# First group of gate products: two weight blocks split under the last plain gate, u's sums in another order, weight sums from their own copy

## The chip, the cores and the metric

The kernel runs on one core of a Trainium2 chip. The metric is the device time of one execution in microseconds; lower is better. A core has TensorE (matrix products, into PSUM), VectorE and ScalarE (elementwise work), GpSimd (called POOL in the profile) and SyncE (called SP), and 16 DMA engines that all queues share. SP and POOL issue nearly all transfers here. A transfer that adds to its target (accumulate) is issued by POOL.

## The reference

One layer of a streaming encoder in float32, 512 frames of 1024 channels. The part that matters here is the merge of three branches:

```python
u = rmsnorm(h, g_mix[l])
proj = u @ w_in[l]
...
y_mem = o_mem.reshape(B, S, MEM_W) @ w_mem_o[l]
gt = jax.nn.sigmoid(gates.reshape(B, S, N_BRANCH, D))
merged = gt[:, :, 0] * y_gla + gt[:, :, 1] * y_fox + gt[:, :, 2] * y_mem
h = h + merged @ w_out[l]
```

The gates are 3 x 1024 columns of `u @ w_in`. A squared-ReLU MLP and a last norm follow.

## The kernel before, in words

**Precision.** Each float32 operand is split into two float32r parts: a ScalarE cast gives hi, a VectorE subtraction gives lo. A product is three matmuls (`mm3`, lines 155 to 157): hi x hi, hi x lo, lo x hi, where the first named is the weight (for a product of u: L155 and L156 read whi, L157 reads wlo). For a block of 128x1024 weights `split_w` does this (cast L145, subtraction L146). `split` (L208, L209) does it for other operands. The raw blocks, whi and wlo each have three buffers that go round, so the cast of a block waits until the third block before it has been used by TensorE.

**Plain gates.** The eight tiles of the FoX gate are plain products `u @ w` with 512 columns (`gT`). The last four run in the GLA stage, woven between the GLA steps by `weave`: after each step, so many units of gate work as its share says (a unit is three matmuls).

**Gate groups.** The other two gates (mem, then gla) are done in four groups of 512 output channels (`gate_group`). Each group replaces an eight-block 2x2 product by a Strassen-Winograd scheme of seven products over half the channels and half the frames, numbered 1 to 7, 24 matmuls of 256 columns each. The left operands are blocks of u (products 1, 2, 4) and sums of them (5, 6, 3, 7, called S1, S2, S4, S3). They are made once, for the first group: `xsum[1]` and `xsum[3]` are computed in the GLA stage (`u_sum`), and `gate_lefts` splits `xsum[1]` into S1 (tiles f0h, f0l), then twice subtracts and adds in place and splits (S2 is f1, S4 is f2), and splits `xsum[3]` into S3, which overwrites a block of u that the plain gates no longer need. The weight operands are blocks ("11", "12", "21", "22") and running sums of them: `total` (wb) starts as 11, and accumulating DMAs make it 11+12, 11+12+22, 11+12+22+21; `other` is 12+22. Each add into `total` must wait until the value before it has been split. Between the products stand the branch's four outputs (`output(j)`: 12 matmuls of 512 columns against `w_mem_o`). `take` sums the products into the gate, `merge` multiplies by the output, and POOL adds to `acc`.

In the first group before, the order on TensorE is 1, 2, output, output, 5, 3, 6, 7, output, 4, output; in the others it is 1, 2, output, 5, output, 3, 6, 7, output, 4, output.

**Who sets the order.** TensorE's order is that of the code. On the other engines and queues a scheduler orders the instructions when the kernel is built; `tc.issue_after(x)` keeps what stands under it behind x. Each engine then works its own list strictly in that order.

**T sums.** `next_sum` hangs a DMA on the cast of every third weight block or so: these make sums of MLP weight blocks in DRAM (tiles T), on POOL's queue.

Of the kernel before, what the change touches and what calls it, by code (L numbers as in the profile page):

```python
# [14 lines left out]
ALU = mybir.AluOpType  # L15
# [49 lines left out]
def hybrid_block(ctx, tc, chunks, wst, memT, xN, cols, gffn, gfin, wup, cst, out):  # L65
    nc = tc.nc
# [24 lines left out]
    def f(ap):  # L91
        return ap.bitcast(F32)
# [27 lines left out]
    chunk_n, cast_now = [0], [None]  # L120

    def next_sum(after):

# [18 lines left out]
    def split_w(raw):  # L142
        hi = wp.tile([P, 1024], F32R, tag="hi", name=nm("whi"))
        lo = wp.tile([P, 1024], F32R, tag="lo", name=nm("wlo"))
        cast = nc.scalar.copy(hi, raw)  # L145
        nc.vector.tensor_tensor(lo, raw, f(hi), op=ALU.subtract)  # L146
# [575 lines left out]
    with pool("gla") as lp:  # L722
# [123 lines left out]
        def u_sum(n):  # L846
# [4 lines left out]
            nc.vector.tensor_tensor(x, x, al, op=ALU.add)  # L851
            nc.vector.tensor_tensor(x, x, bl, op=ALU.subtract)

        xsum = {}
        A11, A12, A21, A22 = ([f(t[:, 4 * k:4 * k + 4, 256 * i:256 * i + 256]) for t in (uhi, ulo)] for i in range(2) for k in range(2))

        steps = (
            (decays, 0, 13), (key_turn, 0, 3), (gla_scores, 0, 3), (states, 0, 3), (gla_scores, 1, 3), (gla_values, 0, 3),
            (gla_values, 1, 3), (decays, 1, 3), (gla_turn, 0, 4), (gla_turn, 1, 4), (key_turn, 1, 3), (gla_scores, 2, 3),
            (states, 1, 3), (u_sum, 1, 0), (gla_scores, 3, 3), (gla_values, 2, 3), (gla_values, 3, 4), (u_sum, 3, 0), (gla_turn, 2, 3),  # L860
            (gla_turn, 3, 3))
        weave([partial(fn, i) for fn, i, _ in steps], 64, *[gla_g(j) for j in range(4)], fox_late(), shares=[n for *_, n in steps])
    gst.close()

# [23 lines left out]
    with pool("outp") as op_:  # L888
# [8 lines left out]
        GATE = {1: [t[:, 0:4, 0:256] for t in (uhi, ulo)], 2: [t[:, 4:8, 0:256] for t in (uhi, ulo)],  # L897
                4: [t[:, 4:8, 256:512] for t in (uhi, ulo)], 5: S1, 6: S2, 3: S4, 7: S3}

        def gate_lefts():  # L900

            split(*S1, xsum[1])
            for to, (ah, al) in ((S2, A11), (S4, A12)):
                nc.vector.tensor_tensor(xsum[1], ah, xsum[1], op=ALU.subtract)
                nc.vector.tensor_tensor(xsum[1], xsum[1], al, op=ALU.add)
                split(*to, xsum[1])
            split(*S3, xsum[3])

        loaded = [None]

        def gate_group(gate, wo, oh, ol, i, lefts=None, last=None):
            src = {b: wst[index["W", gate, i, b]] for b in ("11", "12", "21", "22")}
            total, other = (h_tile(2 * (i % 2) + n, "wb") for n in range(2))
            X = [op_.tile([P, 2, S], F32, tag=f"ct{n}", name=nm("ct")) for n in range(2)]
            (c11, c21), (c12, c22) = ([x[:, :, 256 * n:256 * n + 256] for n in range(2)] for x in X)
            nc.sync.dma_start(total, src["11"])
            first = nc.sync.dma_start(other, src["12"]).ins

            def plus(to, b):
                nc.gpsimd.dma_start(to, src[b], accum_op=ALU.add)  # L920

            def block(b):
                raw = wp.tile([P, 1024], F32, tag="raw", name=nm("raw"))
                with tc.issue_after(first):
                    loaded[0] = nc.sync.dma_start(raw, src[b]).ins
                return raw

            def vec(to, x, y, op=ALU.add):
                nc.vector.tensor_tensor(to, x, y, op=op)

            def tanh(x):
                nc.scalar.activation(x, x, AF.Tanh, scale=0.5)

            def product(n, raw):
                wh, wl = (t.rearrange("p (a k c) -> p a k c", a=2, k=4) for t in split_w(raw))
                uh, ul = GATE[n]
                ps = mmt([P, 2, 256])
                for a in range(2):
                    for k in range(4):
                        mm3(ps[:, a, :], wh[:, a, k, :], wl[:, a, k, :], uh[:, k, :], ul[:, k, :], k == 0, k == 3)  # L940
                return ps

            def take(n, ps):
                if n == 1:
                    nc.scalar.copy(c21, ps)
                if n == 2:
                    vec(c11, c21, ps)
                    tanh(c11)
                if n == 5:
                    nc.scalar.copy(c22, ps)  # L950
                if n == 6:
                    vec(c21, c21, ps, ALU.subtract)
                    vec(c22, c22, c21, ALU.subtract)
                if n == 3:
                    vec(c12, c22, ps)
                    tanh(c12)
                if n == 7:
                    vec(c22, c22, ps, ALU.subtract)
                    tanh(c22)
                    vec(c21, c21, ps)  # L960
                if n == 4:
                    vec(c21, c21, ps)
                    tanh(c21)

            ys = {}

            def output(j):
                if j % 2 == 0:
                    ys["w"] = get_o(wo, j)
# [12 lines left out]
            j = 4 * i  # L982
            take(1, product(1, total))
            plus(total, "12")
            plus(other, "22")
            take(2, product(2, block("21")))
            if lefts is not None:
                lefts()
            output(j + 2)
            if lefts is not None:  # L990
                output(j + 3)
            take(5, product(5, total))
            plus(total, "22")
            if lefts is None:
                output(j + 3)
            p3 = product(3, block("22"))
            take(6, product(6, total))
            plus(total, "21")
            take(3, p3)
            take(7, product(7, other))  # L1000
            merge(j + 2)
            merge(j + 3)
            output(j)
            take(4, product(4, total))
            merge(j)
            output(j + 1)
            merge(j + 1)

        gate_group("gate_mem", "w_mem_o", omh, oml, 0, lefts=gate_lefts)
# [437 lines left out]
```

## Time and profile before

| | |
|---|---|
| median of 3 runs | 852.09 us (850.49 to 853.2) |
| the profiled execution | 849.31 us, span 847.5 us, clock 0.991 |
| TensorE busy | 827.2 us, 98% of the span |
| VectorE, ScalarE, POOL busy | 607.0, 461.2, 107.1 us |
| DMA | 155.61 MB in packets, mean 184 GB/s |
| chain that ended last | TensorE 88%, VectorE 6%, DMA 2% |

A row of a timeline gives start and duration in us, engine, line of the code, operation, output<-input, shape, and in brackets the idle time of the engine before it with what ended it. PE is TensorE, PEld its weight loads, DVE VectorE, ACT ScalarE. Windows give the busy us of each engine in a stretch, then PEclk (the granted TensorE clock as a share of full speed), the busy share of the DMA engines and GB/s. Matmul ends are modelled, so distances between starts say more than durations.

### The profile page before, as it was taken

The numbers are of one execution on the slowest core, as the hardware profiler recorded it, in microseconds if no ns is written. First come the engines' busy times: TensorE is split into PE (matmuls) and PEld (weight loads), VectorE is DVE, ScalarE is ACT, GpSimd is POOL, SyncE is SP. The second block draws the span as 40 slices with busy tenths as digits, with TensorE's granted clock in tenths as the row PEclk, the third lists the DMA queues.
The fourth block names the chain that finished last, engine by engine and source line by source line (L and its number), as shares of the span: only waits on it lengthen the run. The fifth ranks groups of instructions, "written<-read, shape, count | busy, mean of one in ns | idle before, by whom it ended". The sixth has DMA issues, their size and how long they took to land.

```text
span 847.5 us, 12609 instructions
## 1 busy us (share of the span) xinstructions
PE 827.2 (98%) x4841; PEld 723.1 (85%) x4841; DVE 607.0 (72%) x953; ACT 461.2 (54%) x723; POOL 107.1 (13%) x130
## 2 busy tenths in 40 slices
PE   8999999999999999899999999999999999999995
PEld 6888888888888787789999889998998899889984
DVE  5846887665456684764766846887589678877897
ACT  6765777543354231443444535775577467646754
POOL 1000000001002111132422300001001100110011
PEclk9999999999999999999999999999999999999998
DMA  8524654538666474679998531978857875796543
GB/s 312 189 99 151 178 173 124 179 128 238 180 216 159 129 216 120 166 204 234 270 273 213 168 112 33 279 210 192 243 187 157 221 242 165 188 244 201 151 83 116
DMA packets 39181, 155.61 MB, mean 184 GB/s; under 512 B 4880, under 2 KB 5840, under 8 KB 37072
## 3 DMA queue, kind: packets, MB, share of 16 engines
q1 hardware_dynamic: 28144, 96.06, 31.7%
q0 software_dynamic: 9472, 54.53, 30.5%
q10 hardware_dynamic: 1504, 4.21, 1.3%
q8 instruction: 38, 0.62, 0.3%
q14 instruction: 23, 0.19, 0.1%
HBM read 152.65 MB, written 31.49 MB: 217 GB/s over the span
## 4 chain that ended last, share of the span: by engine, by line
PE 88%; DVE 6%; DMA 2%; issue 2%; ACT 1%; POOL 0%; SPq 0%; POOLq 0%; DVEq 0%; ACTq 0%
PE mm L155 22%; PE mm L157 22%; PE mm L156 22%; PE a L156 5%; PE a L155 5%; PE a L157 5%; DVE h L1117 1%; PE a L801 1%; DVE wlo L146 1%; DMA xn<-in_xN_dram 1%; DVE lo L209 1%; DMA wb<-in_wst_dram 1%; PE a L521 1%; DMA raw<-in_wst_dram 1%; PE a L818 1%
## 5 line engine op out<-in xcount | busy, mean ns | idle before, releaser
L155 PE MATMUL mm<-uhi,whi 128*128 128x512 f32 (+1 forms) x352 | 126.9, 360 | 3.1 <-ACT whi L145 3.1
L157 PE MATMUL mm<-uhi,wlo 128*128 128x512 f32 (+1 forms) x352 | 124.6, 354 | 0.9 <-DVE wlo L146 0.9
L156 PE MATMUL mm<-ulo,whi 128*128 128x512 f32 (+1 forms) x352 | 124.4, 353 | 0.0
L146 DVE TENSOR_TENSOR wlo<-raw,whi 128x1024 fp32r<-128x1024 f32 x67 | 87.4, 1308 | 36.9 <-ACT whi L145 36.7
L145 ACT CAST whi<-raw 128x1024 fp32r<-128x1024 f32 x67 | 70.2, 1049 | 67.2 <-PE mm L156 42.5
L208 ACT CAST hi<-raw 128x1024 fp32r<-128x1024 f32 x65 | 68.2, 1049 | 47.4 <-PE mm L156 34.3
L209 DVE TENSOR_TENSOR lo<-raw,hi 128x1024 fp32r<-128x1024 f32 x65 | 79.5, 1223 | 18.7 <-ACT hi L208 18.7
L155 PEld LDWEIGHTS mm<-uhi,whi 128*128 128x128 f32 x352 | 67.3, 191 | 12.6 <-ACT whi L145 3.6
L157 PEld LDWEIGHTS mm<-uhi,wlo 128*128 128x128 f32 x352 | 67.3, 191 | 10.3 <-DVE wlo L146 1.2
L156 PEld LDWEIGHTS mm<-ulo,whi 128*128 128x128 f32 x352 | 67.4, 191 | 8.0
L208 ACT CAST hi<-b 128x1024 fp32r<-128x1024 f32 x40 | 42.0, 1049 | 41.4 <-PE mm L157 26.9
L156 PE MATMUL mm<-lo,ch 128*128 128x512 f32 x160 | 62.5, 391 | 0.9 <-DVE lo L209 0.9
L157 PE MATMUL mm<-u2h,lo 128*128 128x256 f32 x224 | 63.4, 283 | 0.0
L156 PE MATMUL mm<-u2l,hi 128*128 128x256 f32 x224 | 63.4, 283 | 0.0
L155 PE MATMUL mm<-u2h,hi 128*128 128x256 f32 x224 | 63.4, 283 | 0.0
L157 PE MATMUL mm<-hi,cl 128*128 128x512 f32 x160 | 62.3, 389 | 0.0
L155 PE MATMUL mm<-hi,ch 128*128 128x512 f32 x160 | 62.3, 389 | 0.0
L209 DVE TENSOR_TENSOR lo<-b,hi 128x1024 fp32r<-128x1024 f32 x40 | 48.8, 1222 | 18.2 <-ACT hi L208 18.2
L1301 POOL DMA_DIRECT2D b<-in_wst_dram x32 | 27.3, 854 | 272.5 <-DVE lo L209 201.8
L155 PE MATMUL mm<-u2sh,hi 128*128 128x256 f32 x168 | 47.5, 283 | 0.0
L156 PE MATMUL mm<-u2sl,hi 128*128 128x256 f32 x168 | 47.5, 283 | 0.0
L157 PE MATMUL mm<-u2sh,lo 128*128 128x256 f32 x168 | 47.5, 283 | 0.0
(412 smaller groups left out, 2163.5 us busy)
## 6 DMA issues: line engine op xcount, KB each, us to landing
raw<-in_wst_dram SPq DMA_DIRECT2D x113, 512.0 KB
b<-in_wst_dram POOLq DMA_DIRECT2D x32, 512.0 KB, 5.5
raw<-T SPq DMA_DIRECT2D x28, 512.0 KB
T<-in_wst_dram POOLq DMA_DIRECT2D x12, 1024.0 KB, 9.4
wb<-in_wst_dram POOLq DMA_DIRECT2D x16, 512.0 KB, 5.7
b<-in_wst_dram SPq DMA_DIRECT2D x16, 512.0 KB
wb<-in_wst_dram SPq DMA_DIRECT2D x8, 512.0 KB
nFb<-dF ACTq DMA_DIRECT2D x6, 512.0 KB
```

The source lines that it names most:

```text
L145: cast = nc.scalar.copy(hi, raw)
L146: nc.vector.tensor_tensor(lo, raw, f(hi), op=ALU.subtract)
L155: nc.tensor.matmul(ps, lh, rh, start=start, stop=False)
L156: nc.tensor.matmul(ps, lh, rl, start=False, stop=False)
L157: nc.tensor.matmul(ps, ll, rh, start=False, stop=stop)
L208: nc.scalar.copy(hi, src)
L209: return nc.vector.tensor_tensor(lo, src, f(hi), op=ALU.subtract).ins
L521: nc.tensor.matmul(ps[:, :w], q, K[e][:, 0, :w], start=True, stop=False)
L801: nc.tensor.matmul(ps[:, t, :], kk[:, sl], qq[:, sl], start=True, stop=True)
L818: nc.tensor.matmul(po[r, t, :], qpos[e][:, 64 * c:64 * c + 64], prev[:, c, :], start=False, stop=True)
L1117: nc.vector.tensor_tensor(to, to, x, op=op)
L1301: nc.gpsimd.dma_start(to[i], wst[index["B", q, i, x]], accum_op=ALU.add)
```

## The change

It touches the first group alone in its order of work, and a few dependences in all four.

- The first two weight blocks ("11" and "21") are loaded and split in the GLA stage (`gate_ready`, ahead of the last `gla_turn`, with no share of gate work), by SP and with the usual buffers. `ready` hands them to products 1 and 2.
- `total` is still loaded with block 11, as a copy of its own, so its first add doesn't wait for a split.
- `lefts_1` splits S1, then S3; `lefts_2` makes S2 after product 5's split, and S4 after product 6's split.
- The products of the first group come as 1, 2, output, output, 5, 7, 6, output, 3, 4, output.
- Adds are issued in the order of the code, the load of each `w_mem_o` block after the first two loads of its group, and the split of `total` for products 6 and 4 after the cast just before it.
- `decays(1)` has one more share of gate work.

```diff
-        nc.vector.tensor_tensor(lo, raw, f(hi), op=ALU.subtract)
+        low_now[0] = nc.vector.tensor_tensor(lo, raw, f(hi), op=ALU.subtract).ins
...
+        def gate_ready(b):
+            ready.append(get_w(("W", "gate_mem", 0, b)))
...
-            (gla_values, 1, 3), (decays, 1, 3), (gla_turn, 0, 4), (gla_turn, 1, 4), (key_turn, 1, 3), (gla_scores, 2, 3),
+            (gla_values, 1, 3), (decays, 1, 4), (gla_turn, 0, 4), (gla_turn, 1, 4), (key_turn, 1, 3), (gla_scores, 2, 3),
...
-            (gla_turn, 3, 3))
+            (gate_ready, "11", 0), (gate_ready, "21", 0), (gla_turn, 3, 3))
...
-        def gate_lefts():
...
+        def lefts_1():
+            cast = nc.scalar.copy(S1[0], xsum[1]).ins
+            nc.vector.tensor_tensor(S1[1], xsum[1], f(S1[0]), op=ALU.subtract)
+            with tc.issue_after(cast):
+                split(*S3, xsum[3])
+
+        def lefts_2(to, block):
+            with tc.issue_after(low_now[0]):
+                nc.vector.tensor_tensor(xsum[1], block[0], xsum[1], op=ALU.subtract)
+                nc.vector.tensor_tensor(xsum[1], xsum[1], block[1], op=ALU.add)
+                cast = nc.scalar.copy(to[0], xsum[1]).ins
+                nc.vector.tensor_tensor(to[1], xsum[1], f(to[0]), op=ALU.subtract)
+            return cast
...
+            before = summed[0]
             def plus(to, b):
-                nc.gpsimd.dma_start(to, src[b], accum_op=ALU.add)
+                with tc.issue_after(before) if before is not None else ExitStack():
+                    summed[0] = nc.gpsimd.dma_start(to, src[b], accum_op=ALU.add).ins
...
                 if j % 2 == 0:
-                    ys["w"] = get_o(wo, j)
+                    with tc.issue_after(first):
+                        ys["w"] = get_o(wo, j)
...
-            take(1, product(1, total))
+            if ready is None:
+                take(1, product(1, split_w(total)))
             plus(total, "12")
             plus(other, "22")
-            take(2, product(2, block("21")))
-            if lefts is not None:
-                lefts()
+            if ready is not None:
+                take(1, product(1, ready[0]))
+            take(2, product(2, ready[1] if ready else split_w(block("21"))))
+            if ready is not None:
+                with tc.issue_after(low_now[0]):
+                    lefts_1()
             output(j + 2)
...
-            take(5, product(5, total))
+            w = split_w(total)
+            cast = cast_now[0]
+            take(5, product(5, w))
             plus(total, "22")
-            if lefts is None:
+            if ready is not None:
+                cast = lefts_2(S2, A11)
+                p7 = product(7, split_w(other))
+            else:
                 output(j + 3)
-            p3 = product(3, block("22"))
-            take(6, product(6, total))
+                p3 = product(3, split_w(block("22")))
+            with tc.issue_after(cast):
+                w = split_w(total)
+            take(6, product(6, w))
             plus(total, "21")
+            if ready is not None:
+                cast = lefts_2(S4, A12)
+                output(j)
+                p3 = product(3, split_w(block("22")))
             take(3, p3)
```

What the lists of the engines hold at three places, before and now. The first is VectorE at the start of the first group. x_3056 is `xsum[1]`, f0, f1, f2 are S1, S2, S4, wb_3239 is `total`, raw_3277 block 21, raw_3323 the first output's weights. Before:

```order
L209 TENSOR_TENSOR f0l_3234<-x_3056,f0h_3233 128x1024
L146 TENSOR_TENSOR wlo_3246<-wb_3239,whi_3245 128x1024
L904 TENSOR_TENSOR x_3056<-uhi,x_3056 128x1024
L905 TENSOR_TENSOR x_3056<-x_3056,ulo 128x1024
L146 TENSOR_TENSOR wlo_3280<-raw_3277,whi_3279 128x1024
L146 TENSOR_TENSOR wlo_3326<-raw_3323,whi_3325 128x1024
L209 TENSOR_TENSOR f1l_3236<-x_3056,f1h_3235 128x1024
L904 TENSOR_TENSOR x_3056<-uhi,x_3056 128x1024
L905 TENSOR_TENSOR x_3056<-x_3056,ulo 128x1024
L929 TENSOR_TENSOR ct_3241<-ct_3241,mm_3284 128x2x256
```

Now raw_3317 is the first output's weights, wb_3252 `total`, wb_3253 `other`, mm_3286 product 2, mm_3417 product 6, raw_3449 the third output's weights, raw_3468 block 22:

```order
L943 TENSOR_TENSOR ct_3254<-ct_3254,mm_3286 128x2x256
L146 TENSOR_TENSOR wlo_3320<-raw_3317,whi_3319 128x1024
L146 TENSOR_TENSOR wlo_3350<-wb_3252,whi_3349 128x1024
L914 TENSOR_TENSOR x_3056<-uhi,x_3056 128x1024
L146 TENSOR_TENSOR wlo_3385<-wb_3253,whi_3384 128x1024
L915 TENSOR_TENSOR x_3056<-x_3056,ulo 128x1024
L917 TENSOR_TENSOR f1l_3249<-x_3056,f1h_3248 128x1024
L146 TENSOR_TENSOR wlo_3414<-wb_3252,whi_3413 128x1024
L914 TENSOR_TENSOR x_3056<-uhi,x_3056 128x1024
L146 TENSOR_TENSOR wlo_3452<-raw_3449,whi_3451 128x1024
L146 TENSOR_TENSOR wlo_3471<-raw_3468,whi_3470 128x1024
L915 TENSOR_TENSOR x_3056<-x_3056,ulo 128x1024
```

and right behind these:

```order
L943 TENSOR_TENSOR ct_3254<-ct_3254,mm_3417 128x2x256
L943 TENSOR_TENSOR ct_3255<-ct_3255,ct_3254 128x2x256
L917 TENSOR_TENSOR f2l_3251<-x_3056,f2h_3250 128x1024
L146 TENSOR_TENSOR wlo_3509<-wb_3252,whi_3508 128x1024
L943 TENSOR_TENSOR ct_3255<-ct_3255,mm_3474 128x2x256
```

The splits of blocks 11 and 21 have left this place for the GLA stage, the sum of product 2 has moved ahead of the first output's wlo, and the sums of u stand further back, between the splits of weights.

The second place is ScalarE in the same stretch: before, from the last plain gate's tanh on,

```order
L632 ACTIVATE th_3221<-mm_3174 128x512
L208 CAST og_2580<-og_3208 128x512
L208 CAST f0h_3233<-x_3056 128x1024
L145 CAST whi_3245<-wb_3239 128x1024
L145 CAST whi_3279<-raw_3277 128x1024
L145 CAST whi_3325<-raw_3323 128x1024
L208 CAST f1h_3235<-x_3056 128x1024
```

and now from product 1's copy on (mm_3260 is product 1, mm_3353 product 5):

```order
L959 COPY ct_3254<-mm_3260 128x2x256
L145 CAST whi_3319<-raw_3317 128x1024
L946 ACTIVATE ct_3254<-ct_3254 128x2x256
L145 CAST whi_3349<-wb_3252 128x1024
L145 CAST whi_3384<-wb_3253 128x1024
L964 COPY ct_3255<-mm_3353 128x2x256
L916 CAST f1h_3248<-x_3056 128x1024
L145 CAST whi_3413<-wb_3252 128x1024
```

Product 1's cast no longer follows the tanh; the cast of f1 now stands behind the copy of product 5 and ahead of product 6's cast.

The third place is POOL's list between the last GLA norm and the first merges: before,

```order
L215 TENSOR_TENSOR rr_3150<-ms_3149,cst_s 128x4
L920 DMA wb_3240<-in_wst_dram 128x1024
L920 DMA wb_3239<-in_wst_dram 128x1024
L132 DMA T_3_87<-in_wst_dram 16x16384
L920 DMA wb_3555<-in_wst_dram 128x1024
L920 DMA wb_3239<-in_wst_dram 128x1024 x2
```

and now:

```order
L215 TENSOR_TENSOR rr_3150<-ms_3149,cst_s 128x4
L132 DMA T_3_87<-in_wst_dram 16x16384
L934 DMA wb_3252<-in_wst_dram 128x1024
L934 DMA wb_3253<-in_wst_dram 128x1024
L934 DMA wb_3252<-in_wst_dram 128x1024 x2
L934 DMA wb_3557<-in_wst_dram 128x1024
```

The 1 MB copy to T now stands ahead of the first group's adds; wb_3555 and wb_3557 are the next group's `other`. On SP the two early loads stand ahead of the loads of `total` and `other`.

More of the change, by code (lines that the diff above doesn't have):

```diff
@@ L119, in hybrid_block @@
     sums = sum_ops()
-    chunk_n, cast_now = [0], [None]
+    chunk_n, cast_now, low_now = [0], [None], [None]
     def next_sum(after):
@@ L852, in u_sum @@
             nc.vector.tensor_tensor(x, x, bl, op=ALU.subtract)
+        ready = []
+        def gate_ready(b):
+            ready.append(get_w(("W", "gate_mem", 0, b)))
         xsum = {}
@@ L898, in hybrid_block, with gate_group @@
                 4: [t[:, 4:8, 256:512] for t in (uhi, ulo)], 5: S1, 6: S2, 3: S4, 7: S3}
-        def gate_lefts():
[L902 to L911, printed above, removed]
+        def lefts_1():
[10 more added lines that the diff above has]
+            return cast
+        loaded, summed = [None], [None]
+        def gate_group(gate, wo, oh, ol, i, ready=None, last=None):
             src = {b: wst[index["W", gate, i, b]] for b in ("11", "12", "21", "22")}
@@ L932, in tanh, with product @@
                 nc.scalar.activation(x, x, AF.Tanh, scale=0.5)
-            def product(n, raw):
-                wh, wl = (t.rearrange("p (a k c) -> p a k c", a=2, k=4) for t in split_w(raw))
+            def product(n, w):
+                wh, wl = (t.rearrange("p (a k c) -> p a k c", a=2, k=4) for t in w)
                 uh, ul = GATE[n]
@@ L982, in gate_group @@
             j = 4 * i
-            take(1, product(1, total))
+            if ready is None:
+                take(1, product(1, split_w(total)))
             plus(total, "12")
             plus(other, "22")
-            take(2, product(2, block("21")))
-            if lefts is not None:
-                lefts()
+            if ready is not None:
[4 more added lines that the diff above has]
+                    lefts_1()
             output(j + 2)
-            if lefts is not None:
+            if ready is not None:
                 output(j + 3)
-            take(5, product(5, total))
+            w = split_w(total)
+            cast = cast_now[0]
+            take(5, product(5, w))
             plus(total, "22")
-            if lefts is None:
+            if ready is not None:
+                cast = lefts_2(S2, A11)
+                p7 = product(7, split_w(other))
+            else:
                 output(j + 3)
-            p3 = product(3, block("22"))
-            take(6, product(6, total))
+                p3 = product(3, split_w(block("22")))
+            with tc.issue_after(cast):
+                w = split_w(total)
+            take(6, product(6, w))
             plus(total, "21")
+            if ready is not None:
+                cast = lefts_2(S4, A12)
+                output(j)
+                p3 = product(3, split_w(block("22")))
             take(3, p3)
-            take(7, product(7, other))
+            if ready is None:
+                p7 = product(7, split_w(other))
+            take(7, p7)
             merge(j + 2)
             merge(j + 3)
-            output(j)
-            take(4, product(4, total))
+            if ready is None:
+                output(j)
+            with tc.issue_after(cast):
+                w = split_w(total)
+            take(4, product(4, w))
             merge(j)
@@ L1007, in gate_group @@
             merge(j + 1)
-        gate_group("gate_mem", "w_mem_o", omh, oml, 0, lefts=gate_lefts)
+        gate_group("gate_mem", "w_mem_o", omh, oml, 0, ready=ready)
         gate_group("gate_mem", "w_mem_o", omh, oml, 1)
```

## The prediction

> **What bounds the kernel now.** I read the page first, then what TensorE waited for, then the granted clock in steps of 3.41 us around the one place where it waits, then the timelines of the engines there. The page's first rows: TensorE is at work nearly always.
>
> ```profile
> PE 827.2 (98%) x4841; PEld 723.1 (85%) x4841; DVE 607.0 (72%) x953; ACT 461.2 (54%) x723; POOL 107.1 (13%) x130
> ```
>
> So only TensorE's idle time, and time at a lower clock, can be won. The list of TensorE's waits (us in total, times, longest) begins with these two, and both belong to the split of weights into whi and wlo:
>
> ```profile
> PE mm L155 <- ACT whi L145: 4.3, 2, 3.1
> PE mm L157 <- DVE wlo L146: 1.7, 2, 0.9
> ```
>
> 6.0 us, all in the first gate group. Its timeline on TensorE (start, duration, line, shape, idle before):
>
> ```profile
> 338.98 0.39 PE L157 MATMUL mm<-uhi,wlo 128*128 128x512 f32 x1
> 342.51 0.38 PE L155 MATMUL mm<-uhi,whi 128*128 128x256 f32 x1 [3.14 <-ACT whi L145]
> ...
> 343.95 0.39 PE L157 MATMUL mm<-uhi,wlo 128*128 128x256 f32 x1 [0.95 <-DVE wlo L146]
> ...
> 351.07 0.40 PE L155 MATMUL a<-omh,whi 128*128 128x512 f32 x1
> ...
> 356.54 0.28 PE L155 MATMUL mm<-f0h,whi 128*128 128x256 f32 x1
> ...
> 359.41 0.28 PE L155 MATMUL mm<-f2h,whi 128*128 128x256 f32 x1
> ...
> 380.30 0.28 PE L155 MATMUL mm<-uhi,whi 128*128 128x256 f32 x1
> ...
> 411.42 0.28 PE L155 MATMUL mm<-uhi,whi 128*128 128x256 f32 x1
> ```
>
> The last plain gate's last matmul starts at 338.98; 512 columns take 0.23 us (two outputs of 12 from 351.07 to 356.54: 5.47/24), so the group could begin at 339.21. Group 2 begins at 380.30 and group 3 at 411.42. Group 1 thus takes 41.1 us and group 2 31.1, which is what work alone takes: seven products at 2.87 (356.54 to 359.41) and four outputs at 2.73 are 31.0. Group 1 loses 10.1 us: 6.0 of waits, and the rest is clock. The windows (us, busy of PE, PEld, DVE, ACT, POOL, then PEclk, DMA share, GB/s):
>
> ```profile
> 331.04:334.45 3.41, 3.41 (x19) 2.69 (x20) 1.69 (x4) 1.20 (x2) 1.37 (x2) 1.00 0.70 256
> 334.45:337.86 3.41, 3.41 (x20) 2.84 (x19) 2.08 (x6) 1.57 (x2) 0.51 (x1) 1.00 0.78 167
> 337.86:341.28 3.42, 1.50 (x7) 0.90 (x5) 3.11 (x5) 1.82 (x3) 0.00 (x0) 1.00 0.23 46
> 341.28:344.69 3.41, 1.24 (x8) 1.03 (x9) 3.25 (x4) 3.07 (x4) 0.24 (x1) 1.00 0.00 0
> 344.69:348.10 3.41, 3.41 (x19) 3.41 (x18) 3.38 (x4) 1.04 (x1) 2.06 (x3) 0.50 0.62 106
> ...
> 361.76:365.17 3.41, 1.54 (x11) 1.13 (x11) 1.63 (x2) 2.71 (x3) 0.11 (x1) 1.00 0.19 76
> 365.17:368.58 3.41, 3.41 (x19) 3.41 (x18) 1.86 (x2) 0.23 (x1) 0.74 (x1) 0.50 0.62 96
> ```
>
> After a window with 1.24 us of TensorE work, and after one with 1.54, the next runs at clock 0.50 and costs half of 3.41, 1.7 us; twice is 3.4. 6.0 + 3.4 is 9.4 of the 10.1; the rest is the restarts. A window with 1.50 us was not followed by a drop, so the limit is no plain busy time; 11 half-width matmuls stand in the 1.54, 7 full ones in the 1.50.
>
> **The two blocks split under the last plain gate.** Before, the cast for product 1 (whi<-wb) stands in ScalarE's queue behind the last gate's tanh and the first cast of u:
>
> ```profile
> 332.99 0.60 ACT L632 ACTIVATE th<-mm 128x512 f32<-128x512 f32 x1 [0.98 <-PE mm L157]
> ...
> 340.46 1.05 ACT L208 CAST f0h<-x 128x1024 fp32r<-128x1024 f32 x1
> 341.41 1.04 ACT L145 CAST whi<-wb 128x1024 fp32r<-128x1024 f32 x1
> ...
> 348.39 0.59 ACT L945 COPY ct<-mm 128x512 f32<-128x512 f32 x1 [0.96 <-PE mm L157]
> ...
> 362.46 1.99 ACT L145 CAST whi<-wb 128x1024 fp32r<-128x1024 f32 x2 [2.27 <-DMA wb<-in_wst_dram]
> ```
>
> Now both casts (1.05 each, the next 0.95 later) and both subtractions of VectorE (1.22) lie before 339.21. The second needs the whi buffer that the gate ended at 332.95 gives back: cast 332.8 to 333.8, subtraction to 335.1. In the windows from 331.04 to 337.86 ScalarE worked 2.8 of 6.8 us and VectorE 3.8, so 1.05 and 1.22 fit; the rows of gla_values(3) behind the subtraction start 0.8 later (335.0 for 334.2) and end at 336.1, before TensorE's transposes at 336.7. I charge nothing, between 0 and 0.5 if these transposes wait. Product 1 then follows the gate at 339.21 and product 2 at 342.08, ending at 345.1. The waits of 3.14 and 0.95 go, with the clock drop behind them.
>
> **The new order of u's sums and of the products.** Durations and distances on VectorE:
>
> ```profile
> 342.69 1.22 DVE L146 TENSOR_TENSOR wlo<-wb,whi 128x1024 fp32r<-128x1024 f32 x1
> 343.82 1.22 DVE L904 TENSOR_TENSOR x<-uhi,x 128x1024 f32<-128x1024 f32 x1
> 345.07 1.22 DVE L905 TENSOR_TENSOR x<-x,ulo 128x1024 f32<-128x1024 f32 x1
> ...
> 369.25 0.69 DVE L929 TENSOR_TENSOR ct<-ct,mm 128x512 f32<-128x512 f32 x1 [2.22 <-PE mm L157]
> 369.97 0.69 DVE L929 TENSOR_TENSOR ct<-ct,ct 128x512 f32<-128x512 f32 x1
> ```
>
> A wide one follows the last at 1.13, or 1.25 if it needs its result; a narrow one is followed at 0.72. I walk the new queues with them and find three new waits.
>
> (1) First output. Its wlo stands on VectorE behind c11's sum, which needs product 2's end: sum at 345.15, wlo 345.87 to 347.09. TensorE wants it at its third matmul, 344.95 + 0.46 = 345.41. Wait 1.7. The outputs end at 352.1, product 5 at 355.0.
>
> (2) Product 6. ScalarE copies product 5 at 355.2 (0.59), casts f1 (1.05), then whi: 356.6 to 357.7; VectorE subtracts f1 first, then wlo, 357.9 to 359.1. Product 7 hides 2.87 of it: the third matmul of product 6 wants wlo at 358.1. Wait 1.1.
>
> (3) Product 3. VectorE goes on from 357.9: u's first sum (359.0), two wlo (360.2, 361.3), u's second sum (362.4), c21 (363.6), c22 (364.3), f2's subtraction 365.0 to 366.2. TensorE comes from the output at 364.6, its second matmul wants f2l at 364.7. Wait 1.6, ScalarE's f2h (364.8) inside it.
>
> Each lies alone in its stretch of 3.41 us and leaves at least 1.7 us of work there, above the 1.50 that was followed by full clock; I count no drop.
>
> The Trainium skill ("TensorE: Matmul & The Clock Gate", section on what is actually happening) says that the clock halves after an idle window of about 3.4 us, and that the windows run free. By that rule alone no gap here, 3.14 at most, would have cost clock, and the change would be worth the difference of the waits only, 6.0 - 4.4 = 1.6 us. The trace disagrees: its clock fell after windows that were over a third busy.
>
> **The weight sums from their own copy.** The first add into the total no longer waits for product 1's split. POOL issued before, and landing (min, median, max us) was:
>
> ```profile
> 344.45 0.87 POOL L920 DMA_DIRECT2D wb<-in_wst_dram  x1 [9.49 <-issue]
> 345.00 0.84 POOL L132 DMA_DIRECT2D T<-in_wst_dram  x1
> 345.53 1.22 POOL L920 DMA_DIRECT2D wb<-in_wst_dram  x1
> 356.39 0.87 POOL L920 DMA_DIRECT2D wb<-in_wst_dram  x1 [9.65 <-DVE wlo L146]
> ```
>
> ```profile
> DMA to landing us min/median/max: 5.2/6.0/11.2
> ```
>
> In the new order T's copy (1 MB, paced by the cast of the second block, 333.8) goes first, at about 334.1, then both adds at 334.6 and 335.2. Even with the longest row, 11.2, they land at 345.8 and 346.4. The first is wanted by ScalarE at 346.5, the second by 352. So the old second stall goes (the rest of the two totals, 1.2 + 0.8, at the cast of 362.46 that waited for an add) and its clock drop with it. The next adds are issued when the wlo before them ends. Product 5's ends at 348.8, so that add lands at 354.8 by the median, wanted 356.6. Product 6's ends at 359.1: landing 365.1, wanted by ScalarE at 364.8 and by TensorE only at 369.0. Both are hidden. The load of the extra copy, 512 KB, is issued about 295, far ahead of use; if that cover went, it would cost one landing of some 6 us, which I don't expect.
>
> **Sum.** 10.1 lost before, 1.7 + 1.1 + 1.6 = 4.4 after: 5.7 us less. Nothing else on TensorE changes: the products keep number and shape, and one unit of three matmuls moves within the GLA stage. The profiled execution, 849.31 (span 847.5), would become 843.6. The median of the three runs is 852.09, 2.8 above it; I take the same difference from it: 846.4. 0.3%, about what a measurement of this kernel can tell from no change, is 2.6 us.
>
> **The rivals.**
>
> *Adds late.* Three things on the way at 336 (T 1 MB, two adds, and 1.5 MB of SyncE's loads) may hold the adds longer than the longest row. If the first lands at 350 instead of 346, product 5's split ends at 352.4, the next add is issued 3.5 later, lands at 358.4, and product 6 waits 1.9 more. Gain 3.8: 848.3. For it: the landing row goes up to 11.2. Against: its median is 6.0, with a T among its adds. Chance 0.12, of which 0.02 below 2.6.
>
> *The clock falls once more.* One of the three waits falls with others into one free-running window: 1.7 lost, gain 4.0: 848.1. Against: their distance, 10 and 5.5 us. Chance 0.06.
>
> *Given back.* The later groups have little room, so the gain is lost there by waits of TensorE on adds: 852, no change. The group's fourth sum was cast at 402.47, its wlo ready at 404.8, wanted at 406.0: 1.2 us of room.
>
> ```profile
> 402.47 2.00 ACT L145 CAST whi<-wb 128x1024 fp32r<-128x1024 f32 x2 [4.06 <-DMA wb<-in_wst_dram]
> ```
>
> ```profile
> 405.80 0.28 PE L155 MATMUL mm<-uhi,whi 128*128 128x256 f32 x1
> ```
>
> Against: the adds follow TensorE's own pace, since each waits for the split before it, so the room moves along with the group. Chance 0.11, with a change that doesn't do what it says (block 2 split too late) in it.
>
> *Slower.* The DMA engines, not TensorE, set the pace of groups 2 to 4.
>
> ```profile
> 400.00:410.00 10.00, 10.00 (x69) 9.29 (x69) 7.53 (x11) 4.48 (x6) 2.67 (x3) 1.00 1.01 261
> ```
>
> They are full there (share 1.01). If the room of 1.2 us is used up, all 5.7 us come back, the 0.52 MB more cost 2.0 us at 261 GB/s, and one clock drop from the waits 1.7: 852.1 + 3.7 = 855.8. It decides once an add takes over 1.2 us longer than the one before 402.47. Against: no wait of TensorE after 372 stands among the large ones, at that same share. Chance 0.09.
>
> **How the numbers follow.** The forecast has 0.62; its own range is 844.5 to 848.5. Faster: 0.62 + 0.10 + 0.06 = 0.78; same 0.02 + 0.11 = 0.13; slower 0.09. All three new waits gone would give 842.0, the floor; I put the low end at 843.0, and the high end at 850.5, past the late adds and half of what is given back; 852 and 856 stay outside.
>
> **What would show it.** Right: product 1 right behind the last gate; waits of TensorE near 1.7 at the first output (on wlo), 1.1 at product 6, 1.6 at product 3 (on f2l); group 1 near 35.4 us; clock 1.00 throughout. Wrong: a cast of whi that waits for an add beyond 347, a window at 0.50, or TensorE waiting in groups 2 to 4.

## The result, and the profile after

The change makes the kernel faster by 0.6%: 847.06 us (median of 5, 846.24 to 847.15) against 851.9 (850.49 to 853.2); the ratio is 0.9944, 95% interval 0.9929 to 0.9958. The forecast was 846.4. The profiled execution took 846.95 us (span 845.2) against 849.31 (847.5), so the profiles are 2.4 us apart where the medians are 4.8 apart. TensorE's row of the page has as many matmuls as before and is busy for 0.9 us less:

```profile
PE 826.3 (98%) x4841; PEld 721.0 (85%) x4841; DVE 610.0 (72%) x953; ACT 461.3 (55%) x723; POOL 107.2 (13%) x130
```

The list of TensorE's waits (us in total, times, longest). The 3.1 on whi is gone from its head. The second and the last row here are new; the two waits of the third now stand in other places than before:

```profile
PE mm L155 <- ACT hi L267: 1.7, 3, 0.8
PE a L157 <- DVE wlo L146: 1.5, 1, 1.5
PE mm L157 <- DVE wlo L146: 1.5, 2, 0.8
...
PE mm L156 <- DVE f2l L917: 0.9, 1, 0.9
```

Where they stand, on TensorE's timeline (start, duration, line, shape, idle before):

```profile
339.95 0.39 PE L157 MATMUL mm<-uhi,wlo 128*128 128x512 f32 x1
...
348.08 0.50 PE L157 MATMUL a<-omh,wlo 128*128 128x512 f32 x1 [1.52 <-DVE wlo L146]
...
360.26 0.39 PE L157 MATMUL mm<-f1h,wlo 128*128 128x256 f32 x1 [0.75 <-DVE wlo L146]
...
367.26 0.39 PE L156 MATMUL mm<-f2l,whi 128*128 128x256 f32 x1 [0.94 <-DVE f2l L917]
...
375.74 0.28 PE L155 MATMUL mm<-uhi,whi 128*128 128x256 f32 x1
...
402.67 0.39 PE L157 MATMUL mm<-uhi,wlo 128*128 128x256 f32 x1 [0.76 <-DVE wlo L146]
...
471.33 0.39 PE L155 MATMUL a<-whi,mh 128*128 128x512 f32 x1
```

The first row is the last plain gate's last matmul; group 1 could start 0.23 later, at 340.18, and does. It ends at 375.74: 35.56 us instead of 41.09. Groups 2 to 4 end where `w_out` begins, at 471.33; in the kernel before that was here:

```profile
473.85 0.39 PE L155 MATMUL a<-whi,mh 128*128 128x512 f32 x1
```

So the account of the two profiled spans is: ahead of group 1 +0.97 (340.18 for 339.21), group 1 -5.53, groups 2 to 4 +2.04 (95.59 for 93.55), behind them +0.22; in all -2.30. The 0.97 ahead belongs to the execution, not to the change: in its first 20 us the granted clock was 0.83, against 0.91 in the profile before, and e1, e3, e4, e6 and e8, which have the same code up to there and clock 1.00 in those 20 us, could start group 1 between 338.9 and 339.5. The 2.04 is not: the row at 402.67 is its largest piece, a wait in group 2 that the kernel before did not have.

The clock stays at 1.00 in group 1; the two windows with the least work of TensorE are these (columns as in the prediction):

```profile
344.76:348.17 3.41, 1.89 (x15) 1.46 (x13) 1.95 (x3) 1.36 (x3) 0.00 (x0) 1.00 1.06 273
...
365.22:368.63 3.41, 2.44 (x16) 1.78 (x15) 3.11 (x4) 1.71 (x2) 0.00 (x0) 1.00 1.02 239
```

### The profile page after: what moved, and what is told of

The parts are those of the page before. It is cut to its first block, busy times and chain, and to the rows that moved or that the text cites. A ratio compares the mean times of both kernels' runs of the same rounds, so it can differ in the third digit from the quotient of the medians.

```text
span 845.2 us, 12614 instructions
## 1 busy us (share of the span) xinstructions
PE 826.3 (98%) x4841; PEld 721.0 (85%) x4841; DVE 610.0 (72%) x953; ACT 461.3 (55%) x723; POOL 107.2 (13%) x130
## 4 chain that ended last, share of the span: by engine, by line
PE 42%; DVE 5%; DMA 3%; issue 2%; ACT 1%; POOL 0%; POOLq 0%; ACTq 0%; DVEq 0%
PE mm L157 11%; PE mm L156 11%; PE mm L155 11%; DMA wb<-in_wst_dram 3%; PE a L157 3%; PE a L155 3%; PE a L156 3%; DVE wlo L146 1%; DVE h L1152 1%; DVE lo L209 1%; DVE ct L990 1%; DVE ct L943 0%; PE a L1099 0%; DVE cl L209 0%; ACT whi L145 0%
## 5 line engine op out<-in xcount | busy, mean ns | idle before, releaser
L146 DVE TENSOR_TENSOR wlo<-raw,whi 128x1024 fp32r<-128x1024 f32 x68 | 91.6, 1354 | 34.8 <-ACT whi L145 34.7
```

The source lines that it names most:

```text
L146: low_now[0] = nc.vector.tensor_tensor(lo, raw, f(hi), op=ALU.subtract).ins
```

## The experiments

The main theory: the change is worth what it takes from group 1's stalls and the clock drops behind them, less three waits of its own, less something that groups 2 to 4 give back. Rivals: the early split is the whole gain and the order is nothing; the order is; the adds (or the DMA engines) take all of it back. All times are medians; group times come from the one profiled execution, from the point where group 1 could start. Kernels e1, e2, e3, e5 ran beside 29 runs of the kernel before (851.23), e4, e6, e8, e10 beside 23 (851.99), e11 to e14 beside 17 (851.88). The rounds ran on different chips, and the changed kernel ran in the first round only; so a difference of under 1 us between kernels of different rounds says little by itself.

| kernel | us (all runs) | ratio to before, 95% | profiled | group 1 | groups 2-4 |
|---|---|---|---|---|---|
| before | 851.9 (850.5-853.2) | 1 | 849.31 | 41.09 | 93.55 |
| changed | 847.06 (846.2-847.2) | 0.9944 (0.9929-0.9958) | 846.95 | 35.56 | 95.59 |
| e1 old order | 852.36 (849.1-854.0) | 1.0007 (0.9993-1.0021) | 852.65 | 40.16 | 97.70 |
| e2 late split | 849.77 (847.9-853.1) | 0.9987 (0.9971-1.0002) | 849.77 | 38.44 | 96.60 |
| e3 wlo first | 845.27 (845.1-846.1) | 0.9936 (0.9924-0.9948) | 846.05 | 33.74 | 97.79 |
| e5 e2 + filler | 849.87 (847.3-854.5) | 0.9986 (0.9967-1.0005) | 848.42 | 36.96 | 95.90 |
| e4 three waits gone | 843.52 (842.5-843.8) | 0.9906 (0.9891-0.9920) | 842.50 | 31.48 | 96.30 |
| e6 acc on VectorE | 847.45 (846.4-851.3) | 0.9958 (0.9945-0.9972) | 851.26 | 35.55 | 100.84 |
| e8 adds apart | 851.07 (849.1-855.1) | 0.9993 (0.9976-1.0011) | 849.66 | 35.55 | 99.74 |
| e10 T early | 844.20 (843.5-844.9) | 0.9918 (0.9903-0.9933) | 843.81 | 35.60 | 93.40 |
| e11 e4 + e10 | 839.48 (838.8-839.6) | 0.9850 (0.9827-0.9873) | 839.49 | 31.15 | 93.36 |
| e12 before, T early | 848.05 (847.5-852.4) | 0.9957 (0.9940-0.9974) | 852.42 | 43.18 | 93.36 |
| e13 e11, late split | 843.48 (841.5-844.1) | 0.9896 (0.9876-0.9916) | 843.50 | 35.56 | 93.36 |
| e14 e13 + filler | 842.24 (841.9-843.8) | 0.9890 (0.9868-0.9911) | 841.86 | 34.08 | 93.36 |

**e1: the order undone, early split and copy kept.** The part of the edit that concerns u's sums; the rows that put the products back into their old order are left out here.

```diff
-                with tc.issue_after(low_now[0]):
-                    lefts_1()
+                lefts_old()
...
+            split(*S1, xsum[1])
+            for to, (ah, al) in ((S2, A11), (S4, A12)):
+                nc.vector.tensor_tensor(xsum[1], ah, xsum[1], op=ALU.subtract)
+                nc.vector.tensor_tensor(xsum[1], xsum[1], al, op=ALU.add)
+                split(*to, xsum[1])
+            split(*S3, xsum[3])
```

> The changed kernel with one part undone: in the first gate group u's sums and the products stand in the order of the kernel before (f0, then both other sums of u on VectorE, all ahead of product 5; products 1, 2, 5, 3, 6, 7, 4). The early split and the copy of the weight sums stay. My theory, waits by queues: the first output's wlo stands behind c11's sum and one more wide sum of u (wait 2.8 instead of 1.7), product 5's wlo behind f2's subtraction (0.9), and product 6's sum is added so late that its cast waits for it (2.6); 6.3 us of waits against 3.9, group 1 37.4 us against 35.6, the time 1.8 us above the changed kernel, 848.9. Rival, the early split is the whole gain and the order is worth nothing: within 0.5 us of the changed kernel, 847.1. Rival, the order is worth more than the early split: 850 or more.

Measured: 852.36, as slow as the kernel before. TensorE's rows:

```profile
348.40 0.50 PE L157 MATMUL a<-omh,wlo 128*128 128x512 f32 x1 [2.65 <-DVE wlo L146]
...
363.87 0.39 PE L155 MATMUL mm<-f1h,whi 128*128 128x256 f32 x1 [2.38 <-ACT whi L145]
...
365.13 0.39 PE L157 MATMUL mm<-f1h,wlo 128*128 128x256 f32 x1 [0.76 <-DVE wlo L146]
...
379.53 0.28 PE L155 MATMUL mm<-uhi,whi 128*128 128x256 f32 x1
...
407.08 0.39 PE L155 MATMUL mm<-uhi,whi 128*128 128x256 f32 x1 [1.62 <-ACT whi L145]
```

The waits of group 1 add up to what was worked out (with restarts 6.6 us for 6.3), in other shares: 2.65 at the first output, 0.15 at product 5 where 0.9 was expected, 2.38 + 0.76 at product 6. But one window's worth of half clock fell behind the first (0.69 and 0.81 in two windows, 1.7 us), and group 2 waits for its fourth sum (407.08). The reason for both late sums stands on two queues, VectorE's and then POOL's:

```profile
353.29 1.23 DVE L209 TENSOR_TENSOR f2l<-x,f2h 128x1024 fp32r<-128x1024 f32 x1 [1.17 <-ACT f2h L208]
354.44 1.22 DVE L146 TENSOR_TENSOR wlo<-wb,whi 128x1024 fp32r<-128x1024 f32 x1
```

```profile
355.95 0.86 POOL L942 DMA_DIRECT2D wb<-in_wst_dram  x1 [19.26 <-DVE wlo L146]
```

In the changed kernel the same add:

```profile
350.05 0.86 POOL L934 DMA_DIRECT2D wb<-in_wst_dram  x1 [12.54 <-DVE wlo L146]
```

Product 5's wlo is behind f2, so the next add leaves 5.9 us later. The early split without the order is worth nothing here: the rival that makes it the whole gain falls, and the time lies where the other rival had it (850 or more). What kept the old second stall alive was the order of u's sums.

**e2 and e5: the early split undone, and matmuls in the stall.** In e2 both casts stand behind the last gate's tanh; e5 is e2 with this:

```diff
+                    for k in range(8):
+                        end = nc.tensor.matmul(ps, uhi[:, 0, 0:P], uhi[:, 0, :], start=True, stop=True).ins
```

> The changed kernel with the early split undone: the loads of the two blocks stay where they are, but both casts are queued on ScalarE behind the last plain gate's tanh. The order of products and sums and the copy of the weight sums stay. My theory: product 1 waits about 2 us for its whi and 0.9 more for its wlo, as the kernel before did for 3.1 and 0.95, and the clock then falls for one window (1.7); against that the first output's wlo stands ahead of c11's sum on VectorE here, so its wait of 1.7 goes. Group 1 about 38.5 us, the time 849.5 to 851, and no second clock drop, since the adds are not held up by the split. By the Trainium skill's rule (page TensorE: Matmul & The Clock Gate, section on what is actually happening: an idle window of about 3.4 us) no drop: about 848.5. Rival, the order of the sums alone makes the gain: as the changed kernel, 847.1.

> The kernel with the early split undone (e2_late_split), and eight matmuls that nobody reads put on TensorE where it waits for product 1's split (8 x 0.23 = 1.8 us, ended when the cast is). It measures the clock by itself: the waits for the split stay the same, TensorE is at work in them. If idle time in a partly busy window lowers the clock, the half-clock window behind the stall goes and the time falls by about 1.7 us against e2_late_split. If the clock falls after a whole idle window only, there was none, and the time is the same as e2_late_split or up to 0.5 longer.

e2's time came as expected, by another sum (and its interval holds 1, so the order without the early split is not clear of the kernel before either): the scheduler also put `other`'s cast behind product 5's copy, so product 7 waited 1.78 + 0.92 beside product 1's 1.84 + 0.92. e2 is no clean undoing. e5's profile has clock 1.00 through the group where e2's has 0.67 and 0.83, but the medians are the same, which by the expectation speaks against a drop in e2, and the runs spread over 5 and 7 us. Inconclusive; e13 and e14 repeat both without the second stall.

**e3: the first wait taken away.**

```diff
+                with tc.issue_after(low_now[0]):
+                    take(2, p2)
                 output(j + 3)
```

> The changed kernel with one thing added: on VectorE c11's sum stands behind the first output's wlo. My theory: the wait of 1.69 at the first output goes, product 6's wait stays about as it is (its add is issued by a split that does not depend on c11), group 1 33.9 us, the time 1.6 below the changed kernel: 845.5. Rival, given back: the adds of group 1 and 2 don't come earlier, so product 6 or the fourth sum of group 2 waits for the same time longer: 847.1.

Measured 845.27, 1.8 below the changed kernel (by the ratios, 0.9936 against 0.9944, only some 0.7); group 1 33.74 for 33.9. The wait was c11's sum (the one that adds product 2, ahead of the first output's wlo in VectorE's list) and nothing else. In the profiled execution, the slowest of the five, groups 2 to 4 took 97.79, 2.2 more than in the changed kernel: there the gain was given back, as the rival has it, with waits for sums in groups 2 and 4. How much of it the other executions kept is not shown.

**e4: all three taken away, by order alone.** The core of the edit:

```diff
+                with tc.issue_after(low_now[0]):
+                    take(2, p2)
+                p5 = product(5, w)
...
+                with tc.issue_after(cast):
+                    take(5, p5)
...
+                with tc.issue_after(low_now[0]):
+                    cast = nc.scalar.copy(S4[0], xsum[1]).ins
+                    low = nc.vector.tensor_tensor(S4[1], xsum[1], f(S4[0]), op=ALU.subtract).ins
+                with tc.issue_after(low):
+                    take(6, p6)
```

> The changed kernel with its three waits in the first gate group taken away by order alone: c11's sum and tanh stand behind product 5's split; f1's cast stands ahead of product 5's copy on ScalarE; f2's first sum stands ahead of product 6's wlo, its second right behind, f2's subtraction ahead of the sums of c21 and c22 and of product 3's wlo. My theory: the waits are the only loss left in the group, 1.69 + 1.01 + 1.20 = 3.9 us; group 1 31.4 to 32.4 us, the later groups keep the 1.5 us of gaps that they have, and the time is 843 to 844. Rival, the chain of adds is the next bound: product 6, product 4 or the fourth sum of group 2 waits longer by what was won, and the time stays at 845 to 847.

Measured 843.52, group 1 31.48 (work alone is 31.1): the three waits were nearly the whole rest of the group. Groups 2 to 4 still take 96.3.

**e6, e8, e10: what gives the time back in groups 2 to 4.** The four sums of a group (`total` as block 11 alone, then after each of its three adds) are one chain: cast and subtraction of `total`, then the add into it, then the next cast. Casts of such sums on ScalarE in the changed kernel; the first two belong to group 1 (`total` for product 5, then `other` for product 7), the rest are sums 1 to 4 of group 2:

```profile
347.46 1.03 ACT L145 CAST whi<-wb 128x1024 fp32r<-128x1024 f32 x1
349.37 1.05 ACT L145 CAST whi<-wb 128x1024 fp32r<-128x1024 f32 x1 [0.89 <-DMA wb<-in_wst_dram]
...
370.24 1.05 ACT L145 CAST whi<-wb 128x1024 fp32r<-128x1024 f32 x1 [3.13 <-PE mm L156]
380.39 1.05 ACT L145 CAST whi<-wb 128x1024 fp32r<-128x1024 f32 x1 [3.09 <-DMA wb<-in_wst_dram]
389.60 1.05 ACT L145 CAST whi<-wb 128x1024 fp32r<-128x1024 f32 x1 [3.10 <-DMA wb<-in_wst_dram]
...
400.31 2.00 ACT L145 CAST whi<-wb 128x1024 fp32r<-128x1024 f32 x2 [6.30 <-DMA wb<-in_wst_dram]
```

And of the kernel before, group 2's first three (the fourth is the 402.47 of the prediction):

```profile
372.05 1.06 ACT L145 CAST whi<-wb 128x1024 fp32r<-128x1024 f32 x1
383.29 1.05 ACT L145 CAST whi<-wb 128x1024 fp32r<-128x1024 f32 x1 [1.97 <-PE mm L156]
392.99 1.05 ACT L145 CAST whi<-wb 128x1024 fp32r<-128x1024 f32 x1 [5.28 <-DMA wb<-in_wst_dram]
```

From first to fourth cast it is 30.4 us before and 30.1 now, with a group of 31.1: the chain is nearly as long as TensorE's work. Its start is another: 8.25 us ahead of the group before (372.05 for 380.30), 5.50 now (370.24 for 375.74), since it waits for a whi buffer that product 3 gives back, and product 3 now stands directly ahead of product 4. So 2.75 us of lead are gone; the chain made up 0.35 of them, and the fourth cast comes 2.4 us later against the group's start where 1.2 were to spare. That the shorter lead makes the wait is read from these rows; no experiment gave the lead back. Three ways to shorten the chain:

```diff
-                nc.gpsimd.tensor_tensor(acc[j], acc[j], th, op=ALU.add)
+                nc.vector.tensor_tensor(acc[j], acc[j], th, op=ALU.add)
```

> The changed kernel with the sixteen sums of the gated outputs (acc) on VectorE instead of GpSimd. In the changed kernel VectorE's subtraction took 3.64 us instead of 1.22 beside such a sum, and an add was issued 1.1 us after its split had ended, behind such a sum. My theory of what the later groups give back: adds and splits that come late through these sums; then the waits of the fourth sum of group 2 (0.92) and the output of group 4 (0.42) go, and the time is 1 to 1.5 us lower, 845.5 to 846. Rival, the DMA engines set the pace of the adds: the waits stay, 847.1, or up to 1 us more for the 11 us that VectorE has to do on top (16 x 0.69).

```diff
             plus(total, "12")
+            if ready is None:
+                before = summed[0]
             plus(other, "22")
```

> The changed kernel with one thing moved on GpSimd's queue: in groups 2 to 4 the second total's add (needed for product 7 only) stands behind the first total's first add, and no longer runs beside the add for the fourth sum of the group before, which took 8.1 us to its cast there, 6.9 in the kernel before. If two adds at once make the fourth sum late, the wait of 0.92 in group 2 goes, and the time falls by 0.9 to 1.2: 846. Rival, the chain of adds is limited by the bytes as a whole: what the fourth sum wins, the first loses, and the time stays at 847.1, plus or minus 0.3.

```diff
-        op = next(sums, None) if (11 < n < 46 and n % 4 or n > 51 and n % 3 == 0) else None
+        op = next(sums, None) if (11 < n < 44) else None
```

> The changed kernel with the eight last transfers of the weight sums T taken out of the gate groups: the sums are paced by every split from the 12th to the 43rd, so that all 32 are done before the first gate group. The DMA engines have 6 MB or so less to do between 335 and 445, where they were busy 0.91 of the time, and more in the stages ahead, where it was 0.56 to 0.66. If the DMA's pace makes the adds late, the gaps of groups 2 to 4 (0.92 and 0.42 and smaller ones, 2.0 in all against the kernel before) go and the time is 1 to 2 us lower: 845 to 846. Rival: the adds are late through the order on GpSimd and the head start of the chain, and the time stays at 847.1. Rival, slower: the transfers put into the stages ahead make loads late there, 848 or more.

e6: 847.45, nothing won, as its rival had it. It does not clear POOL's sums altogether, since it also gives VectorE 11 us more to do; its profiled execution is the slowest of its twelve, with 100.84 for groups 2 to 4. e8: 851.07, worse than either theory said. Its casts of sums 2, 3 and 4:

```profile
379.05 1.05 ACT L145 CAST whi<-wb 128x1024 fp32r<-128x1024 f32 x1 [3.02 <-DMA wb<-in_wst_dram]
389.90 1.05 ACT L145 CAST whi<-wb 128x1024 fp32r<-128x1024 f32 x1 [3.81 <-DMA wb<-in_wst_dram]
...
399.45 2.00 ACT L145 CAST whi<-wb 128x1024 fp32r<-128x1024 f32 x2 [5.84 <-DMA wb<-in_wst_dram]
```

The fourth step became shorter (9.55 for 10.71), the third longer (10.85 for 9.21): it looks as if an add moved away from one link of the chain lands beside another. e10: 844.20, more than the 1 to 2 us expected, and every gap of groups 2 to 4 is gone (93.40). Windows of the stretch 375 to 472, the changed kernel first, then e10:

```profile
375.00:472.00 97.00, 96.07 (x655) 88.71 (x655) 65.79 (x66) 40.60 (x50) 34.47 (x31) 1.00 0.91 244
```

```profile
375.00:472.00 97.00, 97.00 (x665) 90.50 (x664) 68.51 (x71) 43.65 (x55) 30.75 (x26) 1.00 0.65 173
```

e10's first and fourth cast of group 2, and the add for the fourth on POOL, in e10 and then in the changed kernel:

```profile
369.51 1.05 ACT L145 CAST whi<-wb 128x1024 fp32r<-128x1024 f32 x1 [3.40 <-PE mm L156]
...
398.33 2.00 ACT L145 CAST whi<-wb 128x1024 fp32r<-128x1024 f32 x2 [5.15 <-DMA wb<-in_wst_dram]
```

```profile
391.55 1.75 POOL L934 DMA_DIRECT2D wb<-in_wst_dram  x2 [7.38 <-DVE wlo L146]
```

```profile
392.21 1.78 POOL L934 DMA_DIRECT2D wb<-in_wst_dram  x2 [6.34 <-DVE wlo L146]
```

The DMA engines are busy 0.65 of the time instead of 0.91, the chain takes 28.8 us instead of 30.1, and the same short lead (5.5) is enough. In both kernels the add goes out right behind its split, 2.61 us after the third cast (388.94 in e10, 389.60 above); from there to the fourth cast it is 6.78 us in e10 and 8.10 in the changed kernel. So this add was not late through its place in POOL's list; it landed later, with T's transfers on the same engines. The stages ahead took T's transfers without loss: group 1 could start at 339.42. So the time given back is the chain of adds under the load of T's transfers: without that load nothing is given back.

**e11: e4 and e10 together.**

> Both at once: the three waits of the first group taken away (as e4_three_gone, 3.5 us below the changed kernel) and the sums T ended ahead of the gate groups (as e10_sums_early, 2.9 below). My theory: they are different losses, in group 1 and in groups 2 to 4, and add up to 6.1 or so at most; some of what e4 won it won with the later gaps left (1.7 us), which go now: 840.5 to 841.5, no wait of TensorE over 0.5 us between 338 and 470. Rival, both paid for the same wait: 843.

```profile
339.57 0.28 PE L155 MATMUL mm<-uhi,whi 128*128 128x256 f32 x1
...
370.72 0.28 PE L155 MATMUL mm<-uhi,whi 128*128 128x256 f32 x1
...
464.08 0.39 PE L155 MATMUL a<-whi,mh 128*128 128x512 f32 x1
```

839.48, ratio 0.985 (0.9827 to 0.9873): faster than both kernels and 1 us below the expected range, with 31.15 us for group 1 and no gap on TensorE up to `w_out`. The two losses are separate and add up (7.6 below the changed kernel, 6.4 by the two experiments); where the 1.2 us on top come from is not shown.

**e12: the kernel before with T early.**

> The kernel before with nothing of the change, only the sums T ended ahead of the gate groups. It asks how much of the change was hidden by the later groups. My theory: in the kernel before the later groups have no gaps, so T's going helps it only where an add is waited for in group 1 (2.0 us and the clock drop behind it): 849.5 to 851; against the 844.2 of e10 the change is then worth 5.5 to 6.5, more than the 4.8 that was measured. Rival, T's transfers also make the stalls of the first group: 848 or less, and the change would be worth 4 or less without them.

848.05, 3.8 below the kernel before. My theory falls and the time is the rival's: without T's load the change is worth 3.85 (848.05 to 844.20), less rather than more than the 4.84 with it, though the two differ by no more than rounds do. The kernel before paid for T too, though its profile has no gap in groups 2 to 4; 9 of 12 runs of e12 lie between 847.5 and 848.2, where those of the kernel before go from 849.5 to 856. In which stretch T cost it that is not shown, since its profiled execution is its fastest on record, and e12's profiled one (852.42) is its slowest; that one still has both stalls of the first group (3.14 + 0.95 and 2.28 + 0.46).

**e13 and e14: the price of the first stall, and of its clock.** e11 with the split late, and the same with the eight matmuls.

> e11_three_early with the early split undone alone: both casts stand behind the last plain gate's tanh. No other wait is left beside it, so this is the price of the first stall by itself. My theory: 1.84 for whi and 0.92 for wlo, and a clock drop behind them worth up to 1.7 in those executions where one of the free-running windows falls on the stall; 2.8 to 4.5 us above e11, with a spread of some 1.5 us. Rival, the room in the chain of adds swallows it or the stall costs no clock: 2.8 and no spread.

> e13_late_clean with eight matmuls that nobody reads on TensorE in the wait for product 1's whi (1.8 us, ended when the cast is). The waits for the split stay, TensorE is at work in the first of them. If a stall in a partly busy window lowers the clock, e14 lies below e13 by what the drop costs, up to 1.7 us, and has no half-clock window behind the stall in its profile. If not, e14 is the same as e13 or up to 0.3 longer.

e13 is 4.0 above e11: 2.74 of waits (1.83 and 0.91), and in the profile 1.7 of clock. Windows of e13, then of e14:

```profile
337.86:341.28 3.42, 1.74 (x9) 1.14 (x7) 1.90 (x4) 2.47 (x4) 0.00 (x0) 1.00 0.99 194
341.28:344.69 3.41, 2.65 (x16) 2.45 (x16) 3.41 (x4) 3.41 (x4) 0.00 (x0) 0.77 0.44 142
344.69:348.10 3.41, 3.41 (x24) 3.41 (x23) 2.07 (x2) 1.45 (x3) 0.00 (x0) 0.73 0.67 185
```

```profile
337.86:341.28 3.42, 3.42 (x16) 2.55 (x14) 1.90 (x4) 2.63 (x4) 0.00 (x0) 1.00 0.99 189
341.28:344.69 3.41, 2.65 (x22) 2.57 (x22) 3.41 (x4) 3.32 (x4) 0.00 (x0) 1.00 0.41 153
344.69:348.10 3.41, 3.41 (x29) 3.37 (x28) 3.31 (x4) 1.82 (x3) 0.00 (x0) 1.00 0.59 186
```

0.77 and 0.73 are together half of one window (3.41 x 0.50 = 1.7 us). In e14's profile, with work in the stall, there is no drop and group 1 is 1.48 us shorter (34.08 for 35.56). The medians are 1.24 apart, but the runs overlap: two of e14's five took as long as e13's (843.55 and 843.75), and one of e13's six only 841.46. So the sign rests on one profile of each, and on the like pair e2 and e5; that the filler is what keeps the clock up is likely, not shown. TensorE was never idle for a whole window here: the longest gap in e13 is 1.83 us. The Trainium skill ("TensorE: Matmul & The Clock Gate", section on what is actually happening) gives an idle window of about 3.4 us as what halves the clock; e13's profile, with half a clock behind that gap, does not agree with it.

## Why the prediction was right, point by point

- **First stall.** Right. Product 1 follows the gate at 340.18 and its split is hidden. e13 has the stall by itself, with a cast that comes sooner than in the kernel before: 2.74 of waits and 1.7 of clock, where the sum had 3.14 + 0.95 and 1.7.
- **The three new waits.** Right in place and size: with restarts 1.69, 1.01 and 1.20 (start-to-start), forecast 1.7, 1.1 and 1.6; group 1 35.56 for 35.4. e3 and e4 took away what the queues said, and the waits went.
- **Clock.** Right: 1.00 in group 1.
- **GLA stage.** Charged with nothing; no new wait of TensorE stands there.
- **The old second stall.** It went, but the step gave the reason to the copy of the weight sums. e1 has copy and early split and still waits 2.38 + 0.76 for that sum. The order of u's sums, which lets product 5's split and with it the next add go 5.9 us earlier, is what removed it (e1 puts the products back as well, but product 6 is the third product behind the two outputs in both orders, and the late wlo and add stand in the rows of e1). The copy alone was not undone; what it is worth stays open.
- **Given back.** The step that failed. It said that the adds follow TensorE's own pace, "so the room moves along with the group". The chain follows the whi buffers and its own adds; its lead shrank from 8.25 to 5.50, its fourth sum came 2.4 us later in the group, and the room of 1.2 was overdrawn: 0.92 at the place that the rival named, 2.0 in groups 2 to 4. The rival stood at 0.11 and at 5.7 us; it came true for a third of that. e10 shows the load under which it does: without T's transfers in these groups nothing was given back.
- **Its signs of being wrong.** Of the three that it named, the window at 0.50 did not come. A cast of whi did wait for an add beyond 347 (349.37, for 0.89 us); it cost nothing, since that block, `other`, is wanted by product 7 at 356.1, so the rival of late adds did not come true in group 1. And TensorE did wait in groups 2 to 4.
- **From the profile to the median.** "I take the same difference" (2.8) was wrong: it is 0.1 after. The profiled execution itself was missed by 3.4 us, 846.95 against 843.6 (2.0 given back, 1.0 ahead of group 1, 0.4 in group 1 and behind). The profiled execution of the kernel before was its fastest on record, and the changed kernel's five runs lie within 0.9 us. That the median came within 0.7 is in part luck: what the later groups gave back and the wrong step to the median offset each other.
- **Slower rival.** Its condition (an add over 1.2 us later) was met against the group's start, by 2.4, but the loss in groups 2 to 4 stayed at 2.0 us, not 9: 1.3 in group 2, 0.2 in group 3, 0.6 in group 4. A chain of 30.1 us is still shorter than a group and can catch up; that this is why it stayed small is argued, not shown.

## What to carry to other kernels

When a stall is removed, look for chains off the bounding engine that are nearly as long as its work (here in-place adds, 30.1 of 31.1 us), and work out their lead at the next stage's start, not their pace. Background transfers belong in stages where the DMA engines are free: moving them won 2.9 us here with one line, nearly as much as taking all three waits away by order (3.5). And compare medians with medians: a stalled kernel's single profile can be several us from its usual execution.

## What the hardware showed beyond that

A subtraction of VectorE beside a sum on POOL took up to three times as long. The changed kernel's VectorE, POOL, and the group of all such subtractions (ns, shortest, median, longest):

```profile
375.17 3.64 DVE L146 TENSOR_TENSOR wlo<-raw,whi 128x1024 fp32r<-128x1024 f32 x1
```

```profile
375.01 2.71 POOL L991 TENSOR_TENSOR acc<-acc,ct 128x512 f32<-128x512 f32 x2
```

```profile
L146 DVE TENSOR_TENSOR wlo<-raw,whi x68: 1205/1225/3643, 26.8 to 525.6; 128x1024 fp32r<-128x1024 f32 x68
```

In e6, with those sums on VectorE:

```profile
L146 DVE TENSOR_TENSOR wlo<-raw,whi x68: 1203/1220/1227, 25.4 to 530.0; 128x1024 fp32r<-128x1024 f32 x68
```

The Trainium skill ("SBUF — State Buffer", section "Who interferes with whom") says that a VectorE instruction with two SBUF inputs contends with a GpSimd instruction that reads SBUF; the trace agrees. What it cost this kernel is not shown: e6, without it, was not faster, but has 11 us more work on VectorE.
